# A SwiGLU decoder layer in split fp32: whole-piece splits in the feed-forward part, and seven blocks split in one operation

## Chip, cores and metric

One core of a Trainium2 chip. The metric is the device time of one execution in microseconds; before the change it is 289.91 us, the median of 3 runs (289.13 to 289.95).

## The reference

One decoder layer on 256 tokens of width 1024, in float32: attention with 8 heads of 128 (one block of 256, so plain causal attention), then a SwiGLU feed-forward of 2816 hidden columns, each after an RMS norm and added to the residual, and a last RMS norm.

```python
def rms_norm(x, g):
    y = xf * lax.rsqrt(jnp.mean(xf * xf, axis=-1, keepdims=True) + RMS_EPS)
    return (y * g.astype(jnp.float32)).astype(x.dtype)

def swiglu(h, w_in, w_out):
    g, u = jnp.split(jnp.einsum('bsd,df->bsf', h, w_in), 2, axis=-1)
    return jnp.einsum('bsf,fd->bsd', jax.nn.silu(g) * u, w_out)

x = x + moba_attention(rms_norm(x, attn_norm[j]), attn_w_qkv[j], attn_w_o[j])
x = x + swiglu(rms_norm(x, ffn_norm[i]), ffn_w_in[i], ffn_w_out[i])
return rms_norm(x, final_norm)
```

## The kernel before

**Split numbers.** Every float32 operand of a matmul is split in two fp32r parts: `hi`, which ACT casts (L88, L409, L473), and `lo` = `raw` - `hi`, which DVE subtracts (L89, L410, L474). `mm` (L106) then issues three matmuls on PE: hi with hi, hi with lo, lo with hi. So every weight passes three engines: SP fetches 1 MB (128 x 2048 numbers) into `raw`, ACT casts, DVE subtracts, PE reads. `wpool` (L78) has four buffers each of `raw`, `hi` and `lo`; a cast waits until PE has done with the `hi` of four loads before.

**Order of work.** Attention comes first (L165 to L386); the change does not touch what it does. The feed-forward part (from L390) works on 11 chunks of 256 hidden columns.
- *Input layer.* `hidden(c)` (L440) loads two weight pieces with `load` (L91), which splits each in two halves of 1024, and `gate` (L455) computes silu(g) x u: a step of ACT (L459) and a product of DVE (L460) for each of two row blocks. Chunks 2, 3 and 6, 7 go in pairs through `hidden_two` (L537): its first two loads are `load_sums` (L402), the other two `load`.
- *Seven products.* Where two by two blocks are multiplied, some chunks use seven block products in place of eight (Strassen's scheme in Winograd's form). `load_sums` makes the needed sums of a weight's four blocks on DVE: a double sum (L414), then two single ones (L420, L422), each on the one before. It splits three blocks of the weight itself (1536 columns) in one step and the four sums in two halves of 1024, the first half before the last sum is made.
- *Turning.* The hidden values are turned by DMA: `turn` (L478) copies them to 16-bit planes on ACT (L482) and issues the turn on SP; `join` (L489) copies them back on ACT and splits them into the places that the output layer reads. For the six chunks in SEVEN it splits one block (128 columns), then two (256), then the four sums of blocks (512), three splits in all.
- *Output layer* (L595 to L628). Chunks 0 to 8 in order, 0, 1, 3, 5, 7, 8 with `load_sums` and seven products each into seven accumulators, 2, 4, 6 with `load` and eight products. Chunks 9 and 10 (`TAIL`) are loaded behind them.
- *End* (L632 to L684). DVE and ACT combine the seven accumulators into the residual while PE multiplies chunks 9 and 10, one quarter of the output after the other (`plan`, L648; its last quarter in two parts). Behind each quarter DVE adds it to the residual (L662) and multiplies by the gain (L672), ACT squares and sums (L674); once a row block is whole, ACT takes the root, DVE the reciprocal (L162), both scale (L680, L681) and two DMAs write (L683 on SP, L684 on ACT).

A scheduler sets each engine's order of instructions from dependences and its own estimates; each engine then works strictly in that order. The kernel holds only a few steps in place (`keep_in_program_order`).

Of the kernel before, what the change touches and what calls it, by code (L numbers as in the profile page):

```python
# [26 lines left out]
F32 = mybir.dt.float32  # L27
F32R = mybir.dt.float32r
U16 = mybir.dt.uint16
# [35 lines left out]
def trunk(ctx, tc, xw, x, g2, g3, wqk, wo, w_in, w_out, out):  # L65
# [22 lines left out]
        nc.scalar.copy(hi, raw)  # L88
        nc.vector.tensor_sub(lo, raw, hi.bitcast(F32))  # L89

    def load(src, pieces=2, raw=None):  # L91

        tiles = [early(src) if raw is None else raw]
        tiles += [wpool.tile([P, 2048], F32R, name=n) for n in ("hi", "lo")]
        n = 2048 // pieces
        for i in range(0, 2048, n):
            split_w(*(w[:, i : i + n] for w in tiles))
        return tiles[1:]
# [66 lines left out]
    with tc.tile_pool(name="attn2", bufs=2) as a2:  # L165
# [25 lines left out]
                nc.vector.scalar_tensor_tensor(acc, ss[:, 0:1], 1.0 / D, eps, op0=ALU.mult, op1=ALU.add)  # L191
                r1.append(rstd_of(ss[:, 1:2], f"r1_{k}", acc))
        raws = {h: early(wqk[h]) for h in range(3)}
        wk = {h: load(wqk[h], raw=raws.pop(h)) for h in range(2)}

        pv = [[ps_mm.tile([P, 512], F32, name="pmm") for _ in range(2)] for _ in range(NT)]
        for k in range(KD):
# [131 lines left out]
        for h in range(H):  # L329
            if h > 1:  # L330
                if h + 1 < H:
                    raws[h + 1] = early(wqk[h + 1])
                wk[h] = load(wqk[h], raw=raws.pop(h))
            project(h)
            follow(h)
        nc.sync.dma_start(g2_bc, g2.to_broadcast([P, D]))


        po = [[ps_mm.tile([P, 512], F32, name="pmm") for _ in range(2)] for _ in range(NT)]
        wo_u = [load(wo[i]) for i in range(4)]  # L340

        def wo_mm(h, t, n):
            wh, wl = (w.rearrange("p (k n) -> p k n", k=2)[:, h % 2] for w in wo_u[h // 2])
# [46 lines left out]
    with tc.tile_pool(name="ffn2", bufs=2) as f2:  # L390
# [11 lines left out]
        def load_sums(src, raw=None):  # L402

            raw = early(src) if raw is None else raw
            hi, lo = (wpool.tile([P, 2048], F32R, name=n) for n in ("hi", "lo"))
            rs, hs, ls = weights()

            def part(r, h, l, a, b):
                nc.scalar.copy(h[:, a:b], r[:, a:b])  # L409
                nc.vector.tensor_sub(l[:, a:b], r[:, a:b], h[:, a:b].bitcast(F32))  # L410

            part(raw, hi, lo, 0, 1536)

            nc.vector.tensor_tensor(  # L414
                rs[:, :1024].rearrange("p (a b) -> p a b", a=2),
                raw[:, 512:1536].rearrange("p (a b) -> p a b", a=2),
                raw[:, None, 1536:].to_broadcast([P, 2, 512]),
                op=ALU.add,
            )
            nc.vector.tensor_add(rs[:, 1024:1536], rs[:, :512], raw[:, 1024:1536])  # L420
            part(rs, hs, ls, 0, 1024)
            nc.vector.tensor_add(rs[:, 1536:], rs[:, 1024:1536], raw[:, :512])  # L422
            part(rs, hs, ls, 1024, 2048)
            return hi, lo, hs, ls


# [11 lines left out]
        ahead = {i: early(w_in[i]) for i in range(2)}  # L438

        def hidden(c):  # L440
            u = [load(w_in[i], raw=ahead.pop(i)) for i in (2 * c, 2 * c + 1)]
            pf = [ps_mm.tile([P, 2, 256], F32, name="pmm") for _ in range(NT)]
            order = [(k, t) for k in range(KD) for t in range(NT)]
            if c == 0:
                order.sort(key=lambda kt: kt[1])
            for k, t in order:
                if c == 0 and (k, t) == (0, 1):
                    turn_x1(1, 1)
                wh, wl = (w.rearrange("p (k n) -> p k n", k=4)[:, k % 4] for w in u[k // 4])
                ts = slice(t * P, (t + 1) * P)  # L450
                mm(pf[t].rearrange("p a b -> p (a b)"), x1h[:, k, ts], x1l[:, k, ts], wh, wl, k == 0, k == KD - 1)
            for t in range(NT):
                gate(c, t, pf[t])

        def gate(c, t, gu):  # L455
            if t == 0:
                hs_[c] = f2.tile([P, 2, NT, P], F32, name="hs", bufs=1)
            sg = f2.tile([P, 256], F32, name="sg")
            nc.scalar.activation(sg, gu[:, 0], AF.Silu, scale=r2[t])  # L459
            nc.vector.scalar_tensor_tensor(  # L460
                hs_[c][:, :, t],
                gu[:, 1].rearrange("p (j f) -> p j f", j=2),
                r2[t],
                sg.rearrange("p (j f) -> p j f", j=2),
# [13 lines left out]
        def turn(c):  # L478


            planes = f2.tile([P, 2, 4 * P], U16, name="planes", bufs=1)
            nc.scalar.copy(planes, hs_[c].bitcast(U16).rearrange("p j t (f w) -> p w (j t f)", w=2))  # L482
            turned = f2.tile([P, 2, 4 * P], U16, name="turned")
            turned_[c] = turned
            nc.sync.dma_start_transpose(
# [3 lines left out]
        def join(c):  # L489

            turned = turned_.pop(c)
            ph = f2.tile([P, 2, T], F32, name="ph", bufs=1)

            tc.keep_in_program_order(
                nc.scalar.copy(
                    ph.bitcast(U16).rearrange("p j (t w) -> p (j t) w", w=2), turned.rearrange("p w n -> p n w")
                )
            )
            if c not in SEVEN:
                split(HAT[c], ph)  # L500
                return
            a11, a21, a12, a22 = (ph[:, j, t * P : (t + 1) * P] for j in range(2) for t in range(NT))
            split(HAT[c], ph[:, 0:1, :P])
            split(HAT[c] + P, ph[:, 1:2])
            fs = f2.tile([P, 4, P], F32, name="fs", bufs=1)

            nc.vector.tensor_sub(fs[:, 0], a21, a22)
            nc.vector.tensor_add(fs[:, 1], a11, a21)
            nc.vector.scalar_tensor_tensor(fs[:, 2], fs[:, 0], -1.0, a11, op0=ALU.mult, op1=ALU.subtract)
            nc.vector.tensor_add(fs[:, 3], a12, fs[:, 2])  # L510
            split(HAT[c] + 3 * P, fs)

        assert not {NC - 2, NC - 1} & set(SEVEN) and HAT[NC - 2] + IN7 * 4 * P <= HAT[NC]

# [231 lines left out]
```

## Time and profile before

| what | value |
|---|---|
| median of 3 runs | 289.91 us |
| the profiled execution | 288.93 us |
| its span, first to last instruction | 286.8 us |
| PE (matmul) busy | 278.6 us, 1466 instructions |
| DVE busy | 241.9 us, 377 instructions |
| ACT busy | 209.0 us, 314 instructions |
| DMA | 59.91 MB, mean 209 GB/s |
| mean granted clock of TensorE | 0.996 |

PE is the matmul engine, PEld its weight loads, DVE the vector engine, ACT the scalar engine, SP the one that issues the DMAs here. In a timeline a row gives the start from the beginning of the span, the length, the engine, the line, the operation, what it writes and reads, and in brackets the idle time of the engine before it and what ended that. Numbers of buffers are left out of names, so `lo` stands for every lower part. Two instructions of one engine overlap a little: the next starts before the last has written all. A row with x2 is two that followed each other directly.

### The profile page before, as it was taken

To read this page: it belongs to the slowest core of one execution; us is meant where nothing else is said; L and a number is where in the kernel's file an instruction comes from. 1 tells how busy PE (TensorE), PEld (TensorE's weight loads), DVE (VectorE), ACT (ScalarE), POOL (GpSimd) and SP (SyncE) were. 2 spreads that over 40 slices of the span, in tenths; PEclk is the share of its full clock that TensorE was granted. 3 is DMA by queue.
4 is the path that set the end of the run, shared out by engine and by line. 5 is a ranking of instruction groups with operands and counts; after the bars stand their busy time and mean duration, and the time that the engine had idled before them with its cause. 6 is when DMAs were issued, how large, how long until landed. Compare 5 with 4: busy or idle time off the path is not lost.

```text
span 286.8 us, 3953 instructions
## 1 busy us (share of the span) xinstructions
PE 278.6 (97%) x1466; PEld 238.5 (83%) x1466; DVE 241.9 (84%) x377; ACT 209.0 (73%) x314; POOL 1.3 (0%) x8
## 2 busy tenths in 40 slices
PE   7899999999999999999999999999999999999991
PEld 4688999999988888888888888888888888888881
DVE  3658898867787479997999998989999879999884
ACT  3786879777886469739879869769968596565453
POOL 1000000000000000000000000000000000000000
PEclk9999999999999999999999999999999999999998
DMA  6999694996655422084788754869768276447003
GB/s 203 418 423 418 259 332 74 341 302 206 174 174 171 163 106 77 1 247 130 281 295 266 240 152 125 289 249 303 211 183 250 82 213 252 167 167 264 0 0 146
DMA packets 25506, 59.91 MB, mean 209 GB/s; under 512 B 17424, under 2 KB 17808, under 8 KB 19600
## 3 DMA queue, kind: packets, MB, share of 16 engines
q1 hardware_dynamic: 25200, 59.28, 61.8%
q10 hardware_dynamic: 288, 0.39, 0.4%
q8 instruction: 11, 0.18, 0.3%
q14 instruction: 7, 0.06, 0.1%
HBM read 54.56 MB, written 1.05 MB: 194 GB/s over the span
## 4 chain that ended last, share of the span: by engine, by line
PE 94%; DMA 2%; DVE 1%; ACT 1%; SPq 0%; issue 0%
PE pmm L107 22%; PE pmm L108 22%; PE pmm L109 22%; PE pmm L202 7%; PE pb L107 3%; PE pb L109 3%; PE pb L108 3%; PE pa L107 3%; PE pa L109 3%; PE pa L108 3%; DMA first<-in_xw 2%; PE pb L257 1%; PE pb L315 1%; DVE x_sb L662 0%; SPq L137 0%; DVE xh L672 0%
## 5 line engine op out<-in xcount | busy, mean ns | idle before, releaser
L89 DVE TENSOR_TENSOR lo<-raw,hi 128x1024 fp32r<-128x1024 f32 x70 | 84.2, 1219 | 10.2 <-ACT hi L88 10.0
L88 ACT CAST hi<-raw 128x1024 fp32r<-128x1024 f32 x70 | 71.3, 1049 | 4.0 <-PE pmm L109 3.6
L107 PE MATMUL pmm<-hi,xh 128*128 128x512 f32 x152 | 59.3, 390 | 0.0
L109 PE MATMUL pmm<-hi,xl 128*128 128x512 f32 x152 | 59.1, 389 | 0.0
L108 PE MATMUL pmm<-lo,xh 128*128 128x512 f32 x152 | 59.1, 389 | 0.0
L409 ACT CAST hi<-raw 128x1024 fp32r<-128x1024 f32 (+1 forms) x30 | 35.1, 1193 | 13.8 <-PE pmm L109 3.9
L410 DVE TENSOR_TENSOR lo<-raw,hi 128x1024 fp32r<-128x1024 f32 (+1 forms) x30 | 41.4, 1398 | 3.4 <-ACT hi L409 3.4
L109 PEld LDWEIGHTS pmm<-hi,xl 128*128 128x128 f32 x152 | 28.5, 188 | 6.0
L107 PEld LDWEIGHTS pmm<-hi,xh 128*128 128x128 f32 x152 | 28.5, 188 | 5.9
L108 PEld LDWEIGHTS pmm<-lo,xh 128*128 128x128 f32 x152 | 28.5, 188 | 5.8
L107 PE MATMUL pmm<-hi,first 128*128 128x512 f32 x80 | 31.6, 395 | 0.0
L108 PE MATMUL pmm<-lo,first 128*128 128x512 f32 x80 | 31.2, 391 | 0.0
L109 PE MATMUL pmm<-xh,lo 128*128 128x256 f32 x96 | 27.2, 283 | 0.0
L108 PE MATMUL pmm<-xl,hi 128*128 128x256 f32 x96 | 27.2, 283 | 0.0
L107 PE MATMUL pmm<-xh,hi 128*128 128x256 f32 x96 | 27.1, 283 | 0.0
L109 PEld LDWEIGHTS pmm<-xh,lo 128*128 128x128 f32 x96 | 18.4, 192 | 0.0
L107 PEld LDWEIGHTS pmm<-xh,hi 128*128 128x128 f32 x96 | 18.4, 192 | 0.0
L108 PEld LDWEIGHTS pmm<-xl,hi 128*128 128x128 f32 x96 | 18.4, 192 | 0.0
L107 PEld LDWEIGHTS pmm<-hi,first 128*128 128x128 f32 x80 | 15.0, 188 | 2.9
L108 PEld LDWEIGHTS pmm<-lo,first 128*128 128x128 f32 x80 | 15.0, 188 | 2.9
L459 ACT ACTIVATE sg<-pmm,r 128x256 f32<-128x256 f32 x14 | 6.5, 472 | 11.0 <-PE pmm L109 11.0
L482 ACT COPY planes<-hs 128x1024 uint16<-128x1024 uint16 x11 | 11.5, 1045 | 2.2 <-DVE hs L460 1.6
(183 smaller groups left out, 523.4 us busy)
## 6 DMA issues: line engine op xcount, KB each, us to landing
raw<-in_w_in SPq DMA_DIRECT2D x22, 1024.0 KB, 5.0
raw<-in_w_out SPq DMA_DIRECT2D x11, 1024.0 KB, 4.9
raw<-in_wqk SPq DMA_DIRECT2D x8, 1024.0 KB, 10.8
raw<-in_wo SPq DMA_DIRECT2D x4, 1024.0 KB, 8.2
first<-in_xw SPq DMA_DIRECT2D x3, 640.0 KB, 8.2
second<-in_xw SPq DMA_DIRECT2D x2, 640.0 KB, 11.8
x_sb<-in_x SPq DMA_DIRECT2D x1, 1024.0 KB, 11.1
g_bc<-in_g SPq DMA_DIRECT2D x2, 512.0 KB, 4.8
```

The source lines that it names most:

```text
L88: nc.scalar.copy(hi, raw)
L89: nc.vector.tensor_sub(lo, raw, hi.bitcast(F32))
L107: nc.tensor.matmul(o, lhsT=lh, rhs=rh, start=first, stop=False)
L108: nc.tensor.matmul(o, lhsT=lh, rhs=rl, start=False, stop=False)
L109: nc.tensor.matmul(o, lhsT=ll, rhs=rh, start=False, stop=last)
L202: nc.tensor.matmul(pv[t][a // 512][:, a % 512 : a % 512 + b - a], lhsT=l[:, k, t * P : (t + 1) * P], rhs=r[:, a:b],  start=k == 0 and a % ...
L257: nc.tensor.matmul(ps[:, :P], lhsT=f[:, :P], rhs=f[:, T : T + P], start=True, stop=True)
L315: nc.tensor.matmul(po[:, P:], lhsT=v1[:, hs], rhs=p1, start=False, stop=True)
L409: nc.scalar.copy(h[:, a:b], r[:, a:b])
L410: nc.vector.tensor_sub(l[:, a:b], r[:, a:b], h[:, a:b].bitcast(F32))
L459: nc.scalar.activation(sg, gu[:, 0], AF.Silu, scale=r2[t])
L482: nc.scalar.copy(planes, hs_[c].bitcast(U16).rearrange("p j t (f w) -> p w (j t f)", w=2))
```

## The change

`load` splits its 2048 columns in one piece unless it is told 2; the calls of attention (`wqk`, `wo`) and chunk 0 of the input layer are told 2, so 21 later loads go in one piece. `load_sums` makes all four sums and then splits them in one piece. `join` lays its four blocks and the four sums in one tile of eight, in the order a21, a11, a12, a22, b, d, e, a, and splits the last seven in one operation of 896 columns; the places that the output layer reads keep their order. `gate` writes row block 0 to the middle two blocks and row block 1 to the outer two for these chunks, and `hs` has that order from the start.

```diff
--- before.py
+++ after.py
@@ -88,7 +88,7 @@
         nc.scalar.copy(hi, raw)
         nc.vector.tensor_sub(lo, raw, hi.bitcast(F32))
 
-    def load(src, pieces=2, raw=None):
+    def load(src, pieces=1, raw=None):
 
         tiles = [early(src) if raw is None else raw]
         tiles += [wpool.tile([P, 2048], F32R, name=n) for n in ("hi", "lo")]
@@ -191,7 +191,7 @@
                 nc.vector.scalar_tensor_tensor(acc, ss[:, 0:1], 1.0 / D, eps, op0=ALU.mult, op1=ALU.add)
                 r1.append(rstd_of(ss[:, 1:2], f"r1_{k}", acc))
         raws = {h: early(wqk[h]) for h in range(3)}
-        wk = {h: load(wqk[h], raw=raws.pop(h)) for h in range(2)}
+        wk = {h: load(wqk[h], 2, raws.pop(h)) for h in range(2)}
 
         pv = [[ps_mm.tile([P, 512], F32, name="pmm") for _ in range(2)] for _ in range(NT)]
         for k in range(KD):
@@ -330,14 +330,14 @@
             if h > 1:
                 if h + 1 < H:
                     raws[h + 1] = early(wqk[h + 1])
-                wk[h] = load(wqk[h], raw=raws.pop(h))
+                wk[h] = load(wqk[h], 2, raws.pop(h))
             project(h)
             follow(h)
         nc.sync.dma_start(g2_bc, g2.to_broadcast([P, D]))
 
 
         po = [[ps_mm.tile([P, 512], F32, name="pmm") for _ in range(2)] for _ in range(NT)]
-        wo_u = [load(wo[i]) for i in range(4)]
+        wo_u = [load(wo[i], 2) for i in range(4)]
 
         def wo_mm(h, t, n):
             wh, wl = (w.rearrange("p (k n) -> p k n", k=2)[:, h % 2] for w in wo_u[h // 2])
@@ -418,9 +418,8 @@
                 op=ALU.add,
             )
             nc.vector.tensor_add(rs[:, 1024:1536], rs[:, :512], raw[:, 1024:1536])
-            part(rs, hs, ls, 0, 1024)
             nc.vector.tensor_add(rs[:, 1536:], rs[:, 1024:1536], raw[:, :512])
-            part(rs, hs, ls, 1024, 2048)
+            part(rs, hs, ls, 0, 2048)
             return hi, lo, hs, ls
 
 
@@ -438,7 +437,7 @@
         ahead = {i: early(w_in[i]) for i in range(2)}
 
         def hidden(c):
-            u = [load(w_in[i], raw=ahead.pop(i)) for i in (2 * c, 2 * c + 1)]
+            u = [load(w_in[i], 1 if c else 2, ahead.pop(i)) for i in (2 * c, 2 * c + 1)]
             pf = [ps_mm.tile([P, 2, 256], F32, name="pmm") for _ in range(NT)]
             order = [(k, t) for k in range(KD) for t in range(NT)]
             if c == 0:
@@ -454,11 +453,13 @@
 
         def gate(c, t, gu):
             if t == 0:
-                hs_[c] = f2.tile([P, 2, NT, P], F32, name="hs", bufs=1)
+                hs_[c] = f2.tile([P, 4, P], F32, name="hs", bufs=1)
+
+            b, step = ((t, 2) if c not in SEVEN else (0, 3) if t else (1, 1))
             sg = f2.tile([P, 256], F32, name="sg")
             nc.scalar.activation(sg, gu[:, 0], AF.Silu, scale=r2[t])
             nc.vector.scalar_tensor_tensor(
-                hs_[c][:, :, t],
+                hs_[c][:, b : b + step + 1 : step],
                 gu[:, 1].rearrange("p (j f) -> p j f", j=2),
                 r2[t],
                 sg.rearrange("p (j f) -> p j f", j=2),
@@ -479,7 +480,7 @@
 
 
             planes = f2.tile([P, 2, 4 * P], U16, name="planes", bufs=1)
-            nc.scalar.copy(planes, hs_[c].bitcast(U16).rearrange("p j t (f w) -> p w (j t f)", w=2))
+            nc.scalar.copy(planes, hs_[c].bitcast(U16).rearrange("p b (f w) -> p w (b f)", w=2))
             turned = f2.tile([P, 2, 4 * P], U16, name="turned")
             turned_[c] = turned
             nc.sync.dma_start_transpose(
@@ -489,26 +490,23 @@
         def join(c):
 
             turned = turned_.pop(c)
-            ph = f2.tile([P, 2, T], F32, name="ph", bufs=1)
+            ph = f2.tile([P, 8, P], F32, name="ph", bufs=1)
 
             tc.keep_in_program_order(
                 nc.scalar.copy(
-                    ph.bitcast(U16).rearrange("p j (t w) -> p (j t) w", w=2), turned.rearrange("p w n -> p n w")
+                    ph[:, :4].bitcast(U16).rearrange("p b (t w) -> p (b t) w", w=2), turned.rearrange("p w n -> p n w")
                 )
             )
             if c not in SEVEN:
-                split(HAT[c], ph)
+                split(HAT[c], ph[:, :4])
                 return
-            a11, a21, a12, a22 = (ph[:, j, t * P : (t + 1) * P] for j in range(2) for t in range(NT))
-            split(HAT[c], ph[:, 0:1, :P])
-            split(HAT[c] + P, ph[:, 1:2])
-            fs = f2.tile([P, 4, P], F32, name="fs", bufs=1)
-
-            nc.vector.tensor_sub(fs[:, 0], a21, a22)
-            nc.vector.tensor_add(fs[:, 1], a11, a21)
-            nc.vector.scalar_tensor_tensor(fs[:, 2], fs[:, 0], -1.0, a11, op0=ALU.mult, op1=ALU.subtract)
-            nc.vector.tensor_add(fs[:, 3], a12, fs[:, 2])
-            split(HAT[c] + 3 * P, fs)
+            a21, a11, a12, a22, b, d, e, a = (ph[:, i] for i in range(8))
+
+            nc.vector.tensor_sub(b, a21, a22)
+            nc.vector.tensor_add(d, a11, a21)
+            nc.vector.scalar_tensor_tensor(e, b, -1.0, a11, op0=ALU.mult, op1=ALU.subtract)
+            nc.vector.tensor_add(a, a12, e)
+            split(HAT[c], ph[:, 1:])
 
         assert not {NC - 2, NC - 1} & set(SEVEN) and HAT[NC - 2] + IN7 * 4 * P <= HAT[NC]
```

What the change moves in the built program is seen at three places. The first is PE in the second pair (`hidden_two(6)`), second load of sums; `pa`, `pb` and `pmm` are accumulators, `first` and `third` the split sums of the input, `xh` and `xl` its split self, `hi` and `lo` the split weight.

```order
 L107 MATMUL pa<-hi,first 128x512
+L107 MATMUL pb<-hi,first 128x512 x2
+L107 MATMUL pmm<-hi,xh 128x512
+L108 MATMUL pmm<-lo,xh 128x512
 L108 MATMUL pa<-lo,first 128x512
 L109 MATMUL pa<-hi,third 128x512
-L107 MATMUL pb<-hi,first 128x512
-L108 MATMUL pb<-lo,first 128x512
-L109 MATMUL pb<-hi,third 128x512
-L107 MATMUL pb<-hi,first 128x512
-L108 MATMUL pb<-lo,first 128x512
-L109 MATMUL pb<-hi,third 128x512
```

The first matmul that reads the lower part of the sums (`pa<-lo`) now comes five places behind `pa<-hi` instead of one.

The second is DVE at the last loads, from the double sum of chunk 8 to the first step of the combining. Before:

```order
L414 TENSOR_TENSOR raw<-raw 128x1024
L410 TENSOR_TENSOR lo<-raw,hi 128x1536
L410 TENSOR_TENSOR lo<-raw,hi 128x1024
L420 TENSOR_TENSOR raw<-raw 128x512
L422 TENSOR_TENSOR raw<-raw 128x512
L410 TENSOR_TENSOR lo<-raw,hi 128x1024 x2
L89 TENSOR_TENSOR lo<-raw,hi 128x1024 x4
L634 TENSOR_TENSOR x_sb<-pb,x_sb 128x512
```

With the change:

```order
L414 TENSOR_TENSOR raw<-raw 128x1024
L410 TENSOR_TENSOR lo<-raw,hi 128x2048
L410 TENSOR_TENSOR lo<-raw,hi 128x1536
L420 TENSOR_TENSOR raw<-raw 128x512
L421 TENSOR_TENSOR raw<-raw 128x512
L410 TENSOR_TENSOR lo<-raw,hi 128x2048
L89 TENSOR_TENSOR lo<-raw,hi 128x2048 x2
L632 TENSOR_TENSOR x_sb<-pb,x_sb 128x512
```

The whole lower part of chunk 7's sums now stands ahead of chunk 8's 1536 columns and its sums, where half of it stood behind the 1536; the six halves that were left before the combining are three whole pieces.

The third is DVE at the end, from the last step of the combining to the add of the last part. Before:

```order
L643 TENSOR_TENSOR x_sb<-x_sb,xl 128x512
L662 TENSOR_TENSOR x_sb<-pmm,x_sb 128x512
L669 SCALAR_TENSOR_TENSOR acc<-ss_2608,eps 128x1
L672 TENSOR_TENSOR xh<-x_sb,g_bc 128x512
L662 TENSOR_TENSOR x_sb<-pmm,x_sb 128x512
L162 RECIPROCAL r_0_2628<-r_0_2628 128x1
L672 TENSOR_TENSOR xh<-x_sb,g_bc 128x512
L680 TENSOR_SCALAR xh<-xh,r_0_2628 128x640
L662 TENSOR_TENSOR x_sb<-pa,x_sb 128x512
L669 SCALAR_TENSOR_TENSOR acc<-ss_2649,eps 128x1
L672 TENSOR_TENSOR xh<-x_sb,g_bc 128x256
L662 TENSOR_TENSOR x_sb<-pb,x_sb 128x256
```

With the change (lines two lower):

```order
L641 TENSOR_TENSOR x_sb<-x_sb,xl 128x512
L660 TENSOR_TENSOR x_sb<-pmm,x_sb 128x512
L667 SCALAR_TENSOR_TENSOR acc<-ss_2516,eps 128x1
L660 TENSOR_TENSOR x_sb<-pmm,x_sb 128x512
L670 TENSOR_TENSOR xh<-x_sb,g_bc 128x512 x2
L660 TENSOR_TENSOR x_sb<-pa,x_sb 128x512
L162 RECIPROCAL r_0_2536<-r_0_2536 128x1
L670 TENSOR_TENSOR xh<-x_sb,g_bc 128x256
L678 TENSOR_SCALAR xh<-xh,r_0_2536 128x640
L667 SCALAR_TENSOR_TENSOR acc<-ss_2557,eps 128x1
L660 TENSOR_TENSOR x_sb<-pb,x_sb 128x256
```

The gain product of the second quarter moved from before the third add (`x_sb<-pmm`, the second) to behind it, and the reciprocal and the scaling of the first row block from before the add of `pa` to behind it. On ACT the issue of that block's output DMA (L684, now L682) moved from before the last two squares to between them.

## Rows read from the trace of the kernel before

**Rows 1.** Page, busy time by engine and the chain that ended last.
```profile
PE 278.6 (97%) x1466; PEld 238.5 (83%) x1466; DVE 241.9 (84%) x377; ACT 209.0 (73%) x314; POOL 1.3 (0%) x8
...
PE 94%; DMA 2%; DVE 1%; ACT 1%; SPq 0%; issue 0%
```

**Rows 2.** Busy time by stretch: us, then PE, PEld, DVE, ACT, POOL, granted clock, DMA.
```profile
165.00:175.00 10.00, 10.00 (x46) 8.29 (x45) 10.00 (x16) 7.18 (x11) 0.00 (x0) 1.00 0.43 134
```

**Rows 3.** Groups by shape: operation, shapes, count | busy us, mean ns | idle before.
```profile
L107 PE MATMUL pmm<-hi,xh 128*128 128x512 f32 x152 | 59.3, 390 | 0.0
...
L409 ACT CAST hi<-raw 128x1024 fp32r<-128x1024 f32 x20 | 20.6, 1048 | 8.7 <-DVE raw L422 3.4 <-DVE raw L420 3.0 <-DVE raw L414 1.7
...
L410 DVE TENSOR_TENSOR lo<-raw,hi 128x1536 fp32r<-128x1536 f32 x10 | 17.5, 1753 | 0.8 <-ACT hi L409 0.8
...
L409 ACT CAST hi<-raw 128x1536 fp32r<-128x1536 f32 x10 | 14.8, 1482 | 5.1 <-PE pmm L109 3.3 <-issue 1.1 <-PE pa L109 0.6
...
L89 DVE TENSOR_TENSOR lo<-raw,hi 128x1024 fp32r<-128x1024 f32 x70 | 84.2, 1219 | 10.2 <-ACT hi L88 10.0
...
L420 DVE TENSOR_TENSOR raw<-raw 128x512 f32<-128x512 f32 x10 | 6.9, 686 | 0.1
```

**Rows 4.** Timeline of ACT, second pair: start us, us, what [idle before].
```profile
172.16 0.47 ACT L459 ACTIVATE sg<-pmm,r 128x256 f32<-128x256 f32 x1 [0.20 <-PE pmm L109]
...
173.50 1.05 ACT L482 COPY planes<-hs 128x1024 uint16<-128x1024 uint16 x1
```

**Rows 5.** Timeline of DVE, second pair.
```profile
172.99 0.48 DVE L460 SCALAR_TENSOR_TENSOR hs<-pmm,r,sg 128x256 f32<-128x256 f32 x1
...
175.53 1.23 DVE L410 TENSOR_TENSOR lo<-raw,hi 128x1024 fp32r<-128x1024 f32 x1 [0.33 <-ACT hi L409]
```

**Rows 6.** Timeline of PE, first reads of four lower parts.
```profile
177.62 0.39 PE L108 MATMUL pa<-lo,first 128*128 128x512 f32 x1
...
234.74 0.39 PE L108 MATMUL pb<-lo,first 128*128 128x512 f32 x1
...
267.38 0.39 PE L108 MATMUL pmm<-lo,first 128*128 128x512 f32 x1
...
271.46 0.39 PE L108 MATMUL pb<-lo,first 128*128 128x512 f32 x1
```

**Rows 7.** Timeline of ACT, first cast of chunk 5 of the output layer.
```profile
240.16 1.49 ACT L409 CAST hi<-raw 128x1536 fp32r<-128x1536 f32 x1 [0.65 <-PE pa L109]
```

**Rows 8.** Timeline of DVE, the last loads.
```profile
232.09 2.35 DVE L89 TENSOR_TENSOR lo<-raw,hi 128x1024 fp32r<-128x1024 f32 x2
...
257.08 2.89 DVE L410 TENSOR_TENSOR lo<-raw,hi 128x1536 fp32r<-128x1536 f32 x2
...
259.88 0.69 DVE L420 TENSOR_TENSOR raw<-raw 128x512 f32<-128x512 f32 x1
...
260.60 0.69 DVE L422 TENSOR_TENSOR raw<-raw 128x512 f32<-128x512 f32 x1
...
268.73 0.68 DVE L634 TENSOR_TENSOR x_sb<-pb,x_sb 128x512 f32<-128x512 f32 x1
```

**Rows 9.** Timeline of DVE, the end of the program.
```profile
276.28 0.69 DVE L672 TENSOR_TENSOR xh<-x_sb,g_bc 128x512 f32<-128x512 f32 x1
...
278.24 0.69 DVE L662 TENSOR_TENSOR x_sb<-pmm,x_sb 128x512 f32<-128x512 f32 x1 [1.27 <-PE pmm L109]
...
279.57 0.55 DVE L680 TENSOR_SCALAR xh<-xh,r 128x640 f32<-128x640 f32 x1
...
280.04 0.68 DVE L662 TENSOR_TENSOR x_sb<-pa,x_sb 128x512 f32<-128x512 f32 x1
...
281.11 0.42 DVE L662 TENSOR_TENSOR x_sb<-pb,x_sb 128x256 f32<-128x256 f32 x1
```

**Rows 10.** Timeline of ACT, the end of the program.
```profile
280.22 0.38 ACTq L684 DMA_DIRECT2D out_y<-xh  x1
...
281.62 0.42 ACT L674 ACTIVATE scr<-x_sb 128x256 bf16<-128x256 f32 x1 [0.36 <-DVE acc L669]
```

## Prediction

> **What bounds the kernel now.** I read the page's busy shares and chain first, then busy time by stretch, then groups by shape, then the timelines of PE, ACT and DVE at the joints. The page puts 94% of the chain on PE and 1% each on DVE and ACT [rows 1]. Between 165 and 175 us PE is busy 10.00 of 10.00 us at a granted clock of 1.00, and DVE too has no idle time [rows 2]. In the groups, 152 matmuls of one form have 0.0 us of idle time before them [rows 3]. So from the feed-forward part on PE never waits; 18 matmuls from 267.38 to 271.46 [rows 6] put their starts 0.227 us apart. The change keeps all matmuls. It can win nothing there by making ACT or DVE faster; it can lose wherever a weight piece comes later than PE wants it, and after PE's last matmul, where DVE and ACT end the program.
>
> **What the change saves: nothing on the path.** 21 plain loads and 10 loads with sums lose one split each, and six joins lose two: 43 instructions fewer on ACT and 43 on DVE. On DVE, 512, 1024 and 1536 columns take 686, 1219 and 1753 ns [rows 3]: 0.534 us per 512 columns. A 1536 followed by a 1024 takes 2.89 us together [rows 8], so the first holds DVE for 2.89 - 1.22 = 1.67 us, 0.08 less than it lasts. By the same 0.08 a 512 holds it 0.60 us, of which 0.067 do not grow with the columns. 43 of these are 2.9 us. On ACT 1024 and 1536 take 1048 and 1482 ns [rows 3], 0.434 us per 512, so some 0.09 us fixed once the overlap is off: 3.9 us. PE's matmuls cover both sums. By the same slopes a piece of 2048 lasts 2.29 us on DVE (and holds it 2.20) and 1.92 us on ACT (holds 1.82).
> The Trainium skill (Perfetto Trace Analysis, Optimizing Scalar/DVE Operations) says that grouping into larger operations improves throughput if the engine is saturated, and gives about 60 ns per instruction for DVE on SBUF; an estimate by that page is 43 x 60 ns = 2.6 us gained if DVE were the bound. The trace agrees with the size and not with the condition: DVE is full, but PE does not wait for it [rows 2, 3].
>
> **What it loses: the handover in halves.** DVE could begin the lower part while ACT cast the second half; now it waits for the whole cast, and PE's first use of a load needs the whole of it. I compared, load by load, when the last half is written with the first use of the whole tile.
> - *Plain loads.* The tightest is in the output layer. DVE's two halves run from 232.09 for 2.35 us, to 234.44 [rows 8]; PE first uses that tile at 234.74 [rows 6]. Even unhelped 0.30 us remains: nothing.
> - *Second pair of chunks, second load of sums.* What starts this chain is PE itself: ACT's gate step starts at 172.16, released by PE, and lasts 0.47 [rows 4]. DVE's gate product can start at 172.66 (it started at 172.99, behind another sum [rows 5]) and lasts 0.48. The `planes` copy then starts at 173.17 and holds ACT 0.95 (it lasts 1.05 [rows 4]). The whole cast runs 174.12 to 176.04, the whole lower part 176.07 to 178.36. Before, the second half was written at 175.53 + 1.23 = 176.76 [rows 5]. PE wanted the first lower half at 177.62 [rows 6]; the new PE order puts that matmul four places later, at 177.62 + 4 x 0.227 = 178.53. Some 0.1 us is left if DVE reaches the gate in time. DVE is full until there and now has undivided pieces ahead of it, any of which can make it late. From below: no wait. From above: DVE late by the half of a piece, 0.7 us. I take 0.15, near the lower end, as the chain worked out just fits.
> - *Last loads.* ACT's cast of the first 1536 columns of chunk 5 waits for PE and starts at 240.16, as before [rows 7]. DVE's part of it starts at S = 241.7 (or 241.9, if the sum ahead of it is late). Two sums follow: 1.67 + 0.72 (the second needs the first: 259.88 to 260.60 [rows 8]) + 0.69, so they end at S + 3.08. The whole cast, 1.92 with two handovers of 0.03, keeps DVE idle: lower part at S + 5.06. With 2.20, 2.20 and 1.14 (this load, chunk 6, the double sum of chunk 7) the next 1536 starts at S + 10.60, and by the same sums and cast chunk 7's lower part at S + 15.66. Chunk 8's 1536 starts 2.20 later, its lower part of sums at S + 22.92, ready at S + 25.21 = 266.9 to 267.1; PE wants it at 267.38 [rows 6]. Two more pieces of 2.20 start behind it: the last is ready at S + 29.61 = 271.3 to 271.5; PE wants it at 271.46 [rows 6]. Wait from 0 to 0.4 us (another 0.2 us late at both joints); I take 0.1.
>
> **The end of the program.** After its last weight piece DVE started combining the seven products at 268.73 [rows 8]; now it starts at S + 29.52 = 271.2 to 271.4, some 2.6 us later. Eleven steps of 0.60 and 0.12 for a dependence bring it to 277.9 to 278.2. So DVE's idle 1.27 us before 278.24 [rows 9] is gone, though the add of the second quarter still starts with PE at 278.24. But the order has changed behind it. Before, the product with the gain of the first row's second quarter stood in the idle stretch, at 276.28 [rows 9]; now it stands behind 278.24, and the reciprocal and the 640-column scaling come after the third quarter's add. From 278.24: two adds and two products 4 x 0.60, reciprocal 0.13, a 256 step 0.34, scaling 0.47 (279.57 to 280.04 [rows 9]), one column 0.12: the last add starts at 281.7, where it started at 281.11 [rows 9]. That is **0.6 us** with nothing behind it to cover it. On ACT the issue of the first output DMA, at 280.22 for 0.38 us, stood ahead of the last two squares; now it stands between them, and the last square (at 281.62 [rows 10]) starts at about 282.4 instead of 282.2: 0.2 us more. From both sides: 0.6 if ACT keeps up, 0.9 if all of the issue shows; I take 0.8.
>
> **Other moves** cost nothing. On SP two turns move ahead of weight loads; the releasers in the rows above are ACT and PE, not a DMA. The seven blocks are joined later, but are read only in the output layer, after all hidden chunks. The new block order changes places in scratch tiles only.
>
> **Sum.** 0 + 0.15 + 0.1 + 0.8 = 1.05 us, on the profiled execution's 288.93 us (span 286.8): 290.0. The median of the runs, 289.91, is 0.98 above that execution, so I put the same 1.05 on it: **291.0 us**. A measurement of this kernel can tell about 0.3% from no change, 0.87 us.
>
> **Rivals.**
> - *Not slower: no weight is late* (0.36). Both thin joints hold, and only the end pays, 0.6 to 0.8 us: 290.6, within 0.3%. It decides at 178.53 and 271.46: if the pieces are there before, this is the outcome. For it: both chains worked out just fit. Against: margins of 0.1 us, with DVE full.
> - *Both joints late* (0.17). DVE reaches the gate at 172.66 late by half a piece, 0.7, and the last loads cost 0.4: 289.91 + 0.8 + 1.1 = 291.8.
> - *Faster* (0.07): in runs without the profiler PE may wait for DVE, since the median is 0.98 above the profiled execution. The 2.9 us of DVE's time saved would remove those waits: 289.91 - 0.98 + 0.0 = 288.9 if the end paid nothing. Against: no idle time before a matmul [rows 3], and the end's order is fixed.
> The Trainium skill has this rival's rule in the sentence on grouping in Perfetto Trace Analysis, and in the same section its opposite, that breaking up instructions may let work be completed sooner where these engines hold up others; the handovers above are of the second kind.
>
> **Numbers.** Forecast 0.40, at 291.0; with the rival of both joints, slower by over 0.3%: 0.57. Same 0.36, faster 0.07. The range leaves out the faster case and the far ends: from 289.7 (the lowest run, 289.13, with the end's 0.6) to 292.2 (289.91 + 0.9 + 1.1, and 0.3 for the spread of the runs).
>
> **What would show it.** Right: ACT and DVE with 43 instructions fewer each and 3 to 4 us less busy; PE's idle time small and only at a lower part near 178.5 and 267 to 271.5; DVE idle before its 2048-wide lower parts, released by ACT; DVE's combining starting near 271.3, no idle time before the add at 278.24, the last add 0.6 us later after PE's last matmul than before. Wrong: the last add still right behind PE's last matmul (then the end costs nothing), or PE waiting over 1 us in all (then the joints decide), or a 2048 piece lasting other than 2.29 and 1.92 us.

## The result and the profile after

The change is slower. Its median is 291.21 us (7 runs, 290.55 to 292.29), that of the kernel before beside it 289.19 us (7 runs, 288.22 to 289.95): 2.0 us, ratio 1.0077 with a 95% interval from 1.0058 to 1.0096. Measured again with the experiments it came to 290.40 beside 288.82 us: ratio 1.0058 (1.0041 to 1.0075). The forecast said slower, 291.0 us. It rested on two numbers of which both were off: the base, 289.91 us, was 0.7 above the median of before that was measured beside the change, and the effect, 1.05 us, was half to two thirds of the one measured.

First the page of the change: busy time by engine, and the chain that ended last.

```profile
PE 280.2 (96%) x1466; PEld 239.0 (82%) x1466; DVE 239.4 (82%) x334; ACT 204.4 (70%) x271; POOL 1.3 (0%) x8
...
PE 49%; DVE 25%; DMA 9%; ACT 8%; issue 7%; SPq 0%; ACTq 0%; DVEq 0%
```

Against [rows 1] ACT and DVE have lost 43 instructions each and 4.6 and 2.5 us of work, near what was worked out (3.9 and 2.9). But the chain, 94% PE before, now has DVE with 25% and ACT with 8% in it (25% and 7%, 16% and 5% in two later profiles of the same kernel). The groups by shape (busy us, mean ns, idle time before them and what ended it) say at which handover:

```profile
L410 DVE TENSOR_TENSOR lo<-raw,hi 128x2048 fp32r<-128x2048 f32 x10 | 22.9, 2290 | 8.7 <-ACT hi L409 8.6
L409 ACT CAST hi<-raw 128x2048 fp32r<-128x2048 f32 x10 | 19.1, 1908 | 14.2 <-DVE raw L421 14.2
L89 DVE TENSOR_TENSOR lo<-raw,hi 128x2048 fp32r<-128x2048 f32 x21 | 47.9, 2286 | 1.9 <-ACT hi L88 1.8
```

The ten whole sums are where DVE now stands idle. ACT waits for DVE's last sum, then DVE waits for ACT's whole cast: 8.7 us of idle DVE ahead of ten lower parts, against 1.9 us ahead of the 21 plain ones. The durations, 2.29 and 1.91 us, are those forecast from the slopes of [rows 3].

**Where PE loses the time.** A way to find it: number PE's matmuls in order, take the start of the n-th after and before, and follow the difference, the lag, through the program. It changes only where PE waits in one kernel and not in the other. In the first profiled execution of the change (292.29 us, the slowest of its 7 runs) the lag is 0.15 to 0.20 us from the head of the program on, grows by 1.77 at the second pair and by 1.19 at the last loads, and the last add starts 0.85 us after PE's last matmul, not 0.32: another 0.53. The timeline of PE at the second pair in that execution:

```profile
178.05 0.50 PE L107 MATMUL pa<-hi,first 128*128 128x512 f32 x1 [0.29 <-ACT hi L409]
180.38 0.50 PE L108 MATMUL pa<-lo,first 128*128 128x512 f32 x1 [0.90 <-DVE lo L410]
```

DVE on the way there and at the gate:

```profile
161.16 1.09 DVE L475 TENSOR_TENSOR second<-ph,first 128x896 fp32r<-128x896 f32 x1 [0.75 <-ACT first L474]
...
174.24 0.87 DVE L461 SCALAR_TENSOR_TENSOR hs<-pmm,r,sg 128x256 f32<-128x256 f32 x2
178.03 2.29 DVE L410 TENSOR_TENSOR lo<-raw,hi 128x2048 fp32r<-128x2048 f32 x1 [2.33 <-ACT hi L409]
```

ACT, from 28 us before:

```profile
149.66 1.91 ACT L88 CAST hi<-raw 128x2048 fp32r<-128x2048 f32 x1 [1.77 <-DMA raw<-in_w_in]
...
157.86 1.05 ACT L483 COPY planes<-hs 128x1024 uint16<-128x1024 uint16 x1 [0.99 <-DMA turned<-planes]
```

The forecast of 172.66 was for the second of the gate's two products. In the row at 174.24 that is the later one; it starts at 174.63, 174.43 on the clock of the kernel before, and so is 1.8 us late. The ACT rows say where this begins: a cast waited 1.77 us for a weight load, and 8 us after that the copy to planes another 0.99 us for a turn, both DMAs. Behind that copy DVE waited 0.75 us for the cast of a join's 896 columns, and from that row to the gate it has no idle time in which to catch up. Whether the change makes these DMAs late or this execution did is a question for the experiments.

### The profile page after: what moved, and what is told of

It is laid out like the page before. It is cut to its first block, busy times and chain, and to the rows that moved or that the text cites. A ratio compares the mean times of both kernels' runs of the same rounds, so it can differ in the third digit from the quotient of the medians.

```text
span 290.5 us, 3874 instructions
## 1 busy us (share of the span) xinstructions
PE 280.2 (96%) x1466; PEld 239.0 (82%) x1466; DVE 239.4 (82%) x334; ACT 204.4 (70%) x271; POOL 1.3 (0%) x8
## 3 DMA queue, kind: packets, MB, share of 16 engines
HBM read 54.56 MB, written 1.05 MB: 191 GB/s over the span
## 4 chain that ended last, share of the span: by engine, by line
PE 49%; DVE 25%; DMA 9%; ACT 8%; issue 7%; SPq 0%; ACTq 0%; DVEq 0%
PE pmm L109 11%; PE pmm L108 11%; PE pmm L107 11%; DVE lo L410 8%; PE pmm L202 7%; DVE lo L89 5%; DMA raw<-in_w_out 5%; ACT hi L409 4%; DMA raw<-in_w_in 2%; DVE raw L414 2%; DMA first<-in_xw 2%; PE pa L108 2%; PE pa L109 1%; ACT hi L88 1%; DVE hs L461 1%
## 5 line engine op out<-in xcount | busy, mean ns | idle before, releaser
L89 DVE TENSOR_TENSOR lo<-raw,hi 128x1024 fp32r<-128x1024 f32 (+1 forms) x49 | 81.8, 1678 | 10.3 <-ACT hi L88 10.2
L88 ACT CAST hi<-raw 128x1024 fp32r<-128x1024 f32 (+1 forms) x49 | 68.7, 1418 | 6.1 <-DMA raw<-in_w_in 3.3
L410 DVE TENSOR_TENSOR lo<-raw,hi 128x1536 fp32r<-128x1536 f32 (+1 forms) x20 | 40.2, 2020 | 8.9 <-ACT hi L409 8.8
L409 ACT CAST hi<-raw 128x1536 fp32r<-128x1536 f32 (+1 forms) x20 | 33.6, 1696 | 17.7 <-DVE raw L421 14.2
L414 DVE TENSOR_TENSOR raw<-raw 128x1024 f32<-128x1024 f32 x10 | 12.2, 1221 | 3.0 <-DMA raw<-in_w_out 2.8
```

The costliest lines, as they stand in the source:

```text
L414: nc.vector.tensor_tensor(rs[:, :1024].rearrange("p (a b) -> p a b", a=2), raw[:, 512:1536].rearrange("p (a b) -> p a b", a=2), raw[:, Non ...
```

## The experiments

Four theories to begin with. A: the loss is the handover of the whole sums. B: the 896-column pieces make DVE late at the second pair. C: fewer instructions pay. D: every whole piece costs a little. The kernel before was timed beside each set of kernels, at medians of 288.68, 288.77 and 288.82 us.

**One part alone, and the sums in halves again.**

```diff
-            part(rs, hs, ls, 0, 1024)
             nc.vector.tensor_add(rs[:, 1536:], rs[:, 1024:1536], raw[:, :512])
-            part(rs, hs, ls, 1024, 2048)
+            part(rs, hs, ls, 0, 2048)
```

These lines alone are the first kernel below; `load` with one piece for the 21 loads alone is the second; the order of blocks and the join of seven alone the third; the fourth is the whole change with these lines put back.

> Only the sums of load_sums are split in one piece (10 loads); loads and join as before. Theory A (the whole cast of the sums delays the lower part at the two thin joints, and DVE reaches the end late): nearly all of the loss is here, +1.0 to +2.5 us on the kernel before, with PE waits at the second load of sums of the second pair (near 179 us) and at the last sums (near 268 us), and the last add 0.5 to 0.6 us later behind PE's last matmul. Theory B (at the second pair DVE is late because the join is split in one operation of 896 that waits for ACT): no wait near 179, only the last loads and the end, +0.8 to +1.7 us. Theory C (fewer instructions pay on the path too): no slower.

Measured: 290.06 us, ratio 1.0042 (1.0027 to 1.0056). The lag grows by 0.14 at the second pair, 0.74 at the last loads, and the end is 0.70 later. The whole sums by themselves bring most of the loss.

> Only the 21 plain loads are split in one piece; sums and join as before. Theory A: no wait above 0.3 us anywhere, the order of the end as before, -0.3 to +0.5 us. Theory C: DVE has 21 x 0.067 = 1.4 us less work, so up to 1.4 us faster. Theory D (every whole piece costs, a third of the loss in each part): +0.6 to +1.0 us.

Measured: 289.34 us, ratio 1.0010 (0.9992 to 1.0028): no difference that the runs can tell, though the median stands 0.66 us above that of before. Theory A expected no wait over 0.3 us anywhere. In its profiled execution PE does wait once, at the first read that stood at 234.74 before [rows 6]. The timeline of PE there:

```profile
235.39 0.50 PE L108 MATMUL pb<-lo,first 128*128 128x512 f32 x1 [1.14 <-DVE lo L89]
```

DVE:

```profile
233.04 2.29 DVE L89 TENSOR_TENSOR lo<-raw,hi 128x2048 fp32r<-128x2048 f32 x1 [0.51 <-ACT hi L88]
```

ACT:

```profile
231.09 1.91 ACT L88 CAST hi<-raw 128x2048 fp32r<-128x2048 f32 x1
```

A whole cast of 1.91 and a whole lower part of 2.29 stand one behind the other, and the lag grows by 1.43 us. But the handover is only some 0.4 of this. On the clock of the kernel before (add 0.66 us) the cast starts at 231.75, where it started at 230.74; and what made it 1.0 us late is a weight load on which DVE waited further up. DVE there in this kernel:

```profile
224.83 1.23 DVE L414 TENSOR_TENSOR raw<-raw 128x1024 f32<-128x1024 f32 x1 [1.05 <-DMA raw<-in_w_out]
```

DVE in the kernel before:

```profile
224.47 1.23 DVE L414 TENSOR_TENSOR raw<-raw 128x1024 f32<-128x1024 f32 x1 [0.71 <-DMA raw<-in_w_out]
```

On one clock that is 225.49 against 224.47. With joined blocks and whole sums beside it this place costs 0.0 to 0.05 us in the three profiles of the full change. Whether whole loads alone cost a few tenths in most runs stays open.

> Only the blocks' order and the join in one operation of 896; loads and sums as before. Theory A: no wait, -0.3 to +0.3 us. Theory B: DVE waits about 0.75 us for ACT's cast of 896 before the lower part of a join, and DVE reaches the gate of the second pair later than 173.0 us, with a PE wait near 179 of 0.3 us or more. Theory C: 12 x 0.067 = 0.8 us of DVE's work, up to 0.8 us faster.

Measured: 288.34 us, ratio 0.9987 (0.9969 to 1.0005). No wait of PE from the feed-forward part on that the kernel before does not have.

> The change with the sums split in halves again; loads and join whole. Theory A: the waits near 179 and near 268 us and the late end are gone, -0.3 to +0.8 us on the kernel before. Theory B: the second pair still waits, since loads and join are whole, +0.5 us or more with a PE wait near 179.

Measured: 288.48 us, ratio 0.9993 (0.9975 to 1.0012). Its profile shows no added lag at the second pair or the last loads. With the sums in halves, whole loads and joined blocks together cost nothing and gain nothing that the runs can tell. That is theory A; C and D fall, and B is left only for joined blocks together with whole sums.

**One part back.** Each is the change with one of the other two parts undone, to see whether one of them makes the second pair late.

```diff
-            split(HAT[c], ph[:, 1:])
+            split(HAT[c], ph[:, 0:1, :P])
+            split(HAT[c] + P, ph[:, 1:2])
...
+            split(HAT[c] + 3 * P, fs)
```

> The change with the seven blocks in three operations again (whole sums and whole loads stay). The full change loses 1.8 us of TensorE's time at the second pair, which the whole sums alone do not (0.1 us there), so one of the other two parts makes VectorE late. Theory B (the 896-column pieces do, which VectorE awaits): the second pair goes back to about 0.1 to 0.3, 1.1 us are left at the last loads and 0.5 to 0.7 at the end; 290.0 to 290.6 us beside 288.7. Theory E (the whole loads do: a lower part of 2048 keeps VectorE 2.29 us and its cast ScalarE 1.91 us ahead of the sums): the second pair still costs 1.5 to 2, total 291.0 to 291.6. Theory C (fewer instructions pay): at or under before.

Measured: 289.71 us, ratio 1.0031 (1.0010 to 1.0053); lag 0.01 at the second pair, 1.07 at the last loads, end 0.53. Theory E, 1.5 to 2 us at the second pair, fails; the time lies below the 290.0 that B expected at least.

```diff
-    def load(src, pieces=1, raw=None):
+    def load(src, pieces=2, raw=None):
```

> The change with the plain loads in halves again (whole sums and the joined seven blocks stay). Theory B: the second pair still costs 1.5 to 2 us, the last loads and the end about 1.5 together, 291.0 to 291.6 us beside 288.7. Theory E: the second pair costs 0.1 to 0.3, total 290.0 to 290.6. If neither part alone makes VectorE late there, both this kernel and the one with the old blocks come to 290.0 to 290.6, and the 1.8 us need all three.

Measured: 290.36 us, ratio 1.0044 (1.0023 to 1.0066); 0.48 at the second pair, 0.73 at the last loads, end 0.70. Here B fails, which expected 1.5 to 2 us at the second pair. Neither kernel shows the 1.77 us, so neither part alone makes it. At the last loads whole plain pieces do add to whole sums: 1.07 us here with them and 0.73 without, while the end is 0.53 late with them and 0.70 without.

**Halves in the output layer alone.** The loads and sums of its chunks from the sixth on (5 to 10, six loads) are cut again; all else is the change. The second kernel has halves in the second load of sums of the second pair too.

```diff
-            return load_sums(w_out[c]) if c in SEVEN else load(w_out[c])
+            return load_sums(w_out[c], halves=c >= 5) if c in SEVEN else load(w_out[c], 2 if c >= 5 else 1)
```

> The change with halves for the output layer's loads from the sixth chunk on alone (sums and plain loads), everything else whole. Theory A (the loss is the handover of whole pieces at three places): the 1.1 us at the last loads and the 0.5 at the end go, the 1.8 at the second pair stays: 290.2 to 290.8 us beside 288.7, and VectorE multiplies the last two 512-column pieces one on either side of the add as in the kernel before. Rival F (the lateness won at the second pair runs on to the end whatever the pieces there are): 291.0 or more, waits at the last lower parts still there.

Measured: 288.49 us, ratio 0.9987 (0.9964 to 1.0010): as fast as before, though 25 whole loads and the joined blocks stay. The lag grows by 0.02 at the second pair and by 0.00 at the last loads. Theory A had expected 290.2 to 290.8, as it took the 1.8 us at the second pair to stay; this kernel is the change up to there, and they did not come again. DVE in its trace, from the last sums to the last add:

```profile
261.01 2.36 DVE L410 TENSOR_TENSOR lo<-raw,hi 128x1024 fp32r<-128x1024 f32 x2 [0.94 <-ACT hi L409]
263.29 4.84 DVE L89 TENSOR_TENSOR lo<-raw,hi 128x1024 fp32r<-128x1024 f32 x4
268.05 0.69 DVE L634 TENSOR_TENSOR x_sb<-pb,x_sb 128x512 f32<-128x512 f32 x1
...
277.56 0.69 DVE L662 TENSOR_TENSOR x_sb<-pmm,x_sb 128x512 f32<-128x512 f32 x1 [1.27 <-PE pmm L109]
...
280.43 0.42 DVE L662 TENSOR_TENSOR x_sb<-pb,x_sb 128x256 f32<-128x256 f32 x1
```

With 0.67 us added for the clock of the kernel before, the combining and the end stand as in [rows 8, 9], down to the idle 1.27 us ahead of the add.

> The same and halves also in the second load of sums of the second pair: 5 of the loads with pieces of 2048 are cut again, the other whole ones stay. Theory A: no wait of TensorE over 0.3 us is left at the second pair or at the last loads, the end as in the kernel before: 288.4 to 289.2 us beside 288.7, though it saves nothing either. Theory D (each whole piece costs a little, wherever it stands): 289.6 to 290.4.

Measured: 288.72 us, ratio 0.9992 (0.9970 to 1.0013): nothing more to win at the second pair. (Seven loads are cut again here, not five.)

**The change twice more,** for what was special in the first profiled execution.

> The change itself, once more, for its median beside these kernels and for a second profiled execution. Its first profiled execution, 292.29 us, is the slowest of its runs and has 1.8 us of waits at the second pair, behind a cast of ScalarE that waited 1.77 us for a weight load and 0.99 us for a turn; the kernel with halves in the output layer alone has the same code up to there and no such wait. Theory G (those loads were late in that one execution): in this profile ScalarE waits under 0.6 us for them and TensorE under 0.4 us at the second pair, while 0.6 to 1.2 us at the last loads and 0.4 to 0.8 at the end are there again; median 289.9 to 290.6 us beside 288.7. Theory H (the change makes them late): 1.5 us at the second pair again, 290.8 to 291.5.

> The change a third time, for a third profiled execution: theory G expects no wait of TensorE over 0.4 us at the second pair here either, or one only where a weight load landed late just before; theory H one of 1.5 us. The waits at the last loads and the late end are expected in each of the three.

Measured: 290.40 and, once, 290.19 us. Growth of the lag and lateness of the end in the three profiles, in us:

| kernel | second pair | last loads | end | sum |
|---|---|---|---|---|
| change, first | 1.77 | 1.19 | 0.53 | 3.49 |
| change, second | 0.39 | 1.35 | 0.53 | 2.27 |
| change, third | 0.19 | 1.38 | 0.53 | 2.11 |

Theory H falls, since the 1.5 us at the second pair do not come again. G fits: in the second profile ACT waits for no DMA between 146 and 160 us, and the second pair costs 0.39 us; only the last loads, at 1.35, cost more than the 1.2 us it allowed. The third shows a late load again; ACT lost 1.18 us, and yet TensorE's second pair cost only 0.19:

```profile
148.28 1.91 ACT L88 CAST hi<-raw 128x2048 fp32r<-128x2048 f32 x1 [1.18 <-DMA raw<-in_w_in]
...
155.39 1.05 ACT L483 COPY planes<-hs 128x1024 uint16<-128x1024 uint16 x1
```

Here the turn was in time, and the copy waited for nothing. Over all fourteen profiles ACT waits over 1 us for this load in four: the first and third of the change, the kernel with the sums put back, and the one with chunk 8 in halves below. The second pair costs 1.77, 0.19, 0.00 and 0.31 us there; only in the first does ACT wait for the turn as well. So a late load alone does not make the 1.77 us. That the late turn behind it does is the likely reading; no run forces one, and whether the change makes such a pair of late DMAs more frequent stays open.

**One handover of three cut again.** In the output layer DVE stands idle at whole sums of chunks 5, 7 and 8 for 2.03, 0.93 and 2.05 us in the second profile of the change. The two kernels cut the sums of chunk 5 alone (`halves=c == 5`) and of chunk 8 alone.

> The change with halves in the sums of chunk 5 of the output layer alone. Theory J (VectorE is made late by the whole casts that it awaits, 2.0 us at chunk 5, 0.9 at chunk 7, 2.05 at chunk 8, and what is not won back is late at the end): the idle 2.0 us at chunk 5 are filled, VectorE starts combining 1 to 2 us earlier before TensorE's last matmul than in the change (9.2 to 9.6 us before it), the wait at chunk 8's sums is under 0.3 us: 288.5 to 289.3 us beside 288.7. Rival K (only the last handover, at chunk 8, counts): as the change, 289.9 to 290.6.

Measured: 289.33 us, ratio 1.0026 (1.0007 to 1.0045). No lag is added at the last loads; the end is 0.28 later. Its sums of chunk 8 still cost DVE 2.03 us, but DVE comes to them earlier. The combining starts 9.79 us before PE's last matmul, 0.2 earlier than in the change, where J expected 1 to 2; part of this is that the change's last matmul is itself put off by 1.35 us of waits. And 0.43 us of lag arise elsewhere, between 228 and 233 us, behind a weight load for which DVE waited 1.65 us.

> The change with halves in the sums of chunk 8 of the output layer alone, its last load of sums. Theory J: VectorE stays 0.7 us later at chunk 5 than forecast, but the idle 2.05 us at chunk 8 are filled, so the wait there falls to 0 to 0.5 us and the combining starts 1.5 to 2 us earlier: 288.7 to 289.5 us beside 288.7. Rival K: 288.4 to 289.0, no wait left. Rival F (what is late at chunk 5 stays late): 289.9 to 290.6.

Measured: 289.40 us, ratio 1.0032 (1.0007 to 1.0057). No lag at the last loads either, end 0.04 later; the combining starts 10.60 us before PE's last matmul, 1.0 earlier than in the change, where J expected 1.5 to 2. DVE at chunk 8 and at the start of the combining:

```profile
264.88 0.68 DVE L420 TENSOR_TENSOR raw<-raw 128x512 f32<-128x512 f32 x1
265.48 1.22 DVE L410 TENSOR_TENSOR lo<-raw,hi 128x1024 fp32r<-128x1024 f32 x1
266.62 0.69 DVE L423 TENSOR_TENSOR raw<-raw 128x512 f32<-128x512 f32 x1
267.22 2.29 DVE L89 TENSOR_TENSOR lo<-raw,hi 128x2048 fp32r<-128x2048 f32 x1
...
272.76 0.69 DVE L634 TENSOR_TENSOR x_sb<-pb,x_sb 128x512 f32<-128x512 f32 x1
```

The idle 2.05 us are filled with the first half and a plain piece. Cutting either removes PE's wait at the last loads, so neither handover is the only cause: of the three theories J fits best, and K and F are out. Both medians stand at the upper edge of what J expected or just over it, about 0.5 us above before; the lag that their profiles add from the second pair to the end (0.75 us in the first, 0.35 in the second) is of that size, but which of it is in most runs stays open.

None of the kernels beats the one before by more than the runs can tell.

## Why the prediction came out right, and where it did not

**Sign and place: right.** PE waits at lower parts near 178.5, 267 and 271.5 and, but for 0.05 us, nowhere else in the feed-forward part, DVE is idle ahead of whole lower parts released by ACT, and the end comes later. The saved instructions bought nothing that the runs can tell: the ratios of the kernels with only loads or joins changed, and of the one with sums put back, are 1.0010, 0.9987 and 0.9993, each with 1 in its interval. But one of the prediction's own signs of being wrong came true: PE loses over 1 us in all at the joints (1.7 and 1.6 in the second and third profile), so the joints decide and not the end. The Trainium skill (Perfetto Trace Analysis, Optimizing Scalar/DVE Operations) says that if these engines aren't saturated but cause bubbles on other engines, breaking up instructions may let work be completed sooner; the runs agree (DVE is 82% busy with the change), since cutting six loads again took 1.9 us off the change (290.40 to 288.49, each beside its own 288.8).

**Second pair, 0.15: the chain right, DVE 0.34 us later than taken.** The second profile, DVE, ACT and PE (add 0.42 us for the clock of the kernel before):

```profile
172.18 0.87 DVE L461 SCALAR_TENSOR_TENSOR hs<-pmm,r,sg 128x256 f32<-128x256 f32 x2
...
175.98 2.29 DVE L410 TENSOR_TENSOR lo<-raw,hi 128x2048 fp32r<-128x2048 f32 x1 [2.33 <-ACT hi L409]
```

```profile
174.04 1.91 ACT L409 CAST hi<-raw 128x2048 fp32r<-128x2048 f32 x1
```

```profile
178.33 0.50 PE L108 MATMUL pa<-lo,first 128*128 128x512 f32 x1
```

The second of the two products starts at 172.58, 173.00 on that clock: 0.34 after the forecast 172.66, as DVE has no idle time ahead of it. All behind it is late by as much, the cast at 174.46 (174.12) and the lower part at 176.40 (176.07). It ends at 178.69, PE wanted it at 178.53, and PE loses 0.39. In the kernel with halves in the output layer alone, which is the change up to here, DVE is in time (add 0.69 us):

```profile
171.42 1.04 DVE L463 SCALAR_TENSOR_TENSOR hs<-pmm,r,sg 128x256 f32<-128x256 f32 x2
...
175.38 2.29 DVE L410 TENSOR_TENSOR lo<-raw,hi 128x2048 fp32r<-128x2048 f32 x1 [2.32 <-ACT hi L409]
```

Its second product starts at 171.97, just the 172.66 forecast, its lower part at 176.07, and PE loses 0.02. Over the six profiles whose instructions are the same up to here PE's loss follows that start: 0.02 and 0.05 us at 172.66 and 172.67, 0.19 at 172.81, 0.31 at 172.94, 0.39 at 173.00, and 1.77 at 174.43. The last is 1.8 us late, more than the half piece, 0.7, that stood as the bound. The bound was drawn from DVE's own pieces and left out that a late DMA can hold ACT, and through it DVE.

**Last loads, 0.1: the step that failed.** It was S, the start of DVE's 1536 columns of chunk 5, set at 241.7 by ACT's cast [rows 7]. The second profile of the change, ACT's cast and then DVE (add 0.03 us for the clock of the kernel before):

```profile
240.13 1.49 ACT L409 CAST hi<-raw 128x1536 fp32r<-128x1536 f32 x1 [0.94 <-PE pa L109]
```

```profile
238.79 2.29 DVE L89 TENSOR_TENSOR lo<-raw,hi 128x2048 fp32r<-128x2048 f32 x1
240.99 0.69 DVE L475 TENSOR_TENSOR third<-ph,first 128x512 fp32r<-128x512 f32 x1
241.59 1.22 DVE L414 TENSOR_TENSOR raw<-raw 128x1024 f32<-128x1024 f32 x1
242.73 1.75 DVE L410 TENSOR_TENSOR lo<-raw,hi 128x1536 fp32r<-128x1536 f32 x1
...
247.84 2.29 DVE L410 TENSOR_TENSOR lo<-raw,hi 128x2048 fp32r<-128x2048 f32 x1 [2.03 <-ACT hi L409]
...
265.87 2.29 DVE L410 TENSOR_TENSOR lo<-raw,hi 128x2048 fp32r<-128x2048 f32 x1 [2.05 <-ACT hi L409]
268.08 4.49 DVE L89 TENSOR_TENSOR lo<-raw,hi 128x2048 fp32r<-128x2048 f32 x2
272.49 0.68 DVE L632 TENSOR_TENSOR x_sb<-pb,x_sb 128x512 f32<-128x512 f32 x1
```

S is 242.76, 1.06 late. The cast is done at 241.62, as forecast; but DVE, without idle time, has a whole plain piece and a piece of the join behind it and is only beginning the double sum. This could have been read ahead: in the kernel before DVE was later still. Its rows there:

```profile
242.05 1.22 DVE L414 TENSOR_TENSOR raw<-raw 128x1024 f32<-128x1024 f32 x1
243.18 1.75 DVE L410 TENSOR_TENSOR lo<-raw,hi 128x1536 fp32r<-128x1536 f32 x1
```

The cast of [rows 7] was done at 241.65 there, and DVE's part of it started 1.5 us after. The forecast let the change remove all of that; it removed 0.4. From S on the chain was good: S + 25.21 was forecast for the lower part of chunk 8's sums, S + 25.43 is measured (265.87 + 2.29 + 0.03 - 242.76). So it is ready at 268.19, 0.81 after PE wanted it [rows 6], and PE shows it:

```profile
267.13 0.39 PE L107 MATMUL pmm<-hi,first 128*128 128x512 f32 x1
268.22 0.50 PE L108 MATMUL pmm<-lo,first 128*128 128x512 f32 x1 [0.71 <-DVE lo L410]
268.56 0.39 PE L109 MATMUL pmm<-hi,third 128*128 128x512 f32 x1
...
272.63 0.50 PE L108 MATMUL pb<-lo,first 128*128 128x512 f32 x1
```

With the second wait, at 272.63, it comes to 1.35 us instead of 0.1. The rival of both late joints allowed 0.4 here.

**End, 0.8: the 0.6 right (0.53), the 0.2 nothing.** The second profile, DVE:

```profile
279.56 0.69 DVE L660 TENSOR_TENSOR x_sb<-pmm,x_sb 128x512 f32<-128x512 f32 x1 [0.19 <-PE pmm L109]
280.16 1.28 DVE L670 TENSOR_TENSOR xh<-x_sb,g_bc 128x512 f32<-128x512 f32 x2
281.37 0.68 DVE L660 TENSOR_TENSOR x_sb<-pa,x_sb 128x512 f32<-128x512 f32 x1
...
282.96 0.42 DVE L660 TENSOR_TENSOR x_sb<-pb,x_sb 128x256 f32<-128x256 f32 x1
```

From the add that PE releases to the last add 3.40 us, forecast 3.46 (278.24 to 281.7), before 2.87 [rows 9]. PE's last matmul starts at 282.11. Behind the last add both kernels take 5.7 us to the end (288.7 - 282.96; 286.8 - 281.11), so the output DMA's issue on ACT cost nothing. What lies under the order is DVE's lateness: with the old order the product of 0.60 would stand in 0.19 us of idle time, and the add would start 0.41 late instead. By this sum the order itself is worth only 0.1; no run forced the old order. Over all profiles the two go together: where the combining starts 12.06 us or more before PE's last matmul, the last add follows it by 0.31 or 0.32; at 10.60 by 0.36, at 9.79 by 0.59, at 9.6 by 0.85, at 9.15 by 1.02.

**Plain loads, 0: right in the full change, with wrong working.** The sum for 234.74 took the end of the two old halves, 234.44, and left out that a whole lower part also waits for a whole cast; the kernel with whole loads alone shows 1.43 us of lag in one profile, some 0.4 of it from the handover.

**Together.** 0 + 0.3 + 1.36 + 0.53 = 2.2 us by the second and third profile (0.39 and 0.19 make the 0.3), against 1.05 forecast and 2.0 and 1.6 measured. The forecast had 0.8 of its 1.05 at the end and 0.25 at the joints; the profiles have 0.5 and 1.7, nearer in kind to the rival of both late joints. That the forecast time was still near is chance: a base 0.7 too high made up for most of an effect 1.0 too small.

## What to carry to other kernels

A larger operation saves its fixed cost on its own engine, but where two engines hand a tile on, it turns their overlap into a sum: here up to 2.05 us of idle DVE per load of sums for 0.07 us saved on it. Judge this where the slack is thin and nothing follows in which it could be won back, at the end of the program above all; cutting six of 31 loads again was enough. And when a chain is worked out from where an engine starts, check what that engine has in front of it, not only what releases it; the row of the kernel before shows it.

## What was not expected of the hardware

- A wait of PE costs more than its length. The matmul behind a wait lasts 0.50 us instead of 0.39, and the next starts 0.34 behind it instead of 0.227 (268.22 to 268.56 above, at a granted clock of 1.00): 0.11 us each time. The profile models the ends of matmuls, so the starts are the sounder sign.
- The idle time of DVE at a whole sum, where it has nothing else to do, is the cast and 0.14 us: 263.13 + 0.69 to a cast from 263.93 for 1.91 us, and the lower part at 265.87.
- In four of the fourteen profiles PE lost 0.9 to 2.5 us in attention, whose instructions are the same in all these kernels, and the head of the program varied by 1.3 us. One profiled execution can so differ from another by as much as the whole effect; the lag, taken stretch by stretch, separates the two.
